# RWKV-7 layer on one core: separate decay loads, heads stacked alike and half-row Gram products in the recurrence, with re-timed planner tables

## The chip, the cores and the metric

The kernel runs on one core of a Trainium2 chip. The metric is the device time of one execution in microseconds, median of the runs; lower is better. The engines are named as in the profile: PE is TensorE, DVE VectorE, ACT ScalarE, POOL GpSimd, SP SyncE, which here only issues DMAs.

## The reference, cut to what matters

One layer (DEPTH is 1) over 2048 tokens of width 1024: RWKV-7 time mixing with 16 heads of 64, a LayerNorm, then a gated MLP of width 2816 with a causal convolution of width 3, and a second LayerNorm. The part that the change touches is the recurrence over time:

```python
def step(state, inp):
    r_t, w_t, k_t, v_t, kk_t, a_t = inp
    sa = jnp.einsum('bhij,bhj->bhi', state, -kk_t)
    state = (state * w_t[:, :, None, :]
             + sa[..., None] * (kk_t * a_t)[:, :, None, :]
             + v_t[..., None] * k_t[:, :, None, :])
    return state, jnp.einsum('bhij,bhj->bhi', state, r_t)
```

`w_t` is a decay per channel, the exponential of a negative decay log. All is float32.

## The kernel before

The program is one list of nodes. Each node has an engine, a cost in us (`dur`), a due time (`prio`), the nodes it depends on, and the buffers that it takes and gives back. A planner in the Python code (`Plan.order`) plays this list through with these costs, at each moment starts on a free engine the ready node with the lowest due time, and writes the instructions out in that order. On the chip each engine runs its own instructions strictly in the order written. So the numbers in `pl.add(engine, cost, due, ...)` and in the tables TS, TW and TF set the order in which instructions stand; they cost no time by themselves. A changed cost in one phase can reorder another, since the plan is one.

There are four phases, which overlap at their borders: the projections (A, to about 700 us), the recurrence (S, about 700 to 1280), the output projection with LayerNorm (W, to about 1490), and the MLP (F, four blocks of 512 tokens, to the end).

The recurrence goes over 16 tiles `t` of 128 tokens; a tile has two chunks `c` of 64 tokens and two halves `h` of 8 heads, and heads are taken in pairs, `e` being the even or the odd one. Per half:

- One DMA loads `l`, 128 x 5 x 512: r, kp, kkn, b and th (the decay logs); there is one buffer for it. PE sums the decay logs along the chunk (`csI`), and ACT makes three exponentials, `P`, `Pe` and `Pi`.
- DVE multiplies kkn by `Pe` (line 875) and r by `P` (line 879), PE transposes both (`tr`) and ACT writes them to `AR`. PE also transposes the whole of `P` (`pcp`), of which only two columns per pair, the chunk decays, are kept in `PC`.
- DVE multiplies b and kp by `Pi` into `BKn` (line 928). For even heads b lies in partitions 0 to 63 and kp in 64 to 127, for odd heads the other way round, so each multiply is split by `e`: 64 x 256 elements, in blocks of 64. PE transposes `BKn` (`tb`), and ACT copies each head's 64 rows into one of two tiles `BKT`, whose other 64 rows are kept zero; there is one pair of them.
- PE makes the Gram products `G`, 128 contraction rows of which 64 are zero, and DVE masks them into `Gm` (line 955).

Per tile DVE then inverts 64 small triangular matrices, 31 steps of a multiply and an add (lines 990 and 995), between DMAs that regroup them (`NU`, `NUs`, `XD`, `XT`). Per chunk follow the serial steps: ACT copies the state to `UV`, PE makes `Z`, `SA`, `dS` and the output `Y`, and DVE updates `stmp` (line 1141) and `state` (line 1146).

Of W this matters: for each tile ACT takes squares, DVE makes a reciprocal root (line 1295 and twelve short operations of lines 173 to 178), scales and gates (`wE`, lines 1312 and 1315), PE transposes (`tr`, line 1338), ACT and DVE split the result (`yH`, `yL`), and PE multiplies it into `z`. In F, PE alternates between `ps` (first matrix, weights split by DVE into `wiL`, line 1594) and `acc` (second matrix, weights split into `woL`, line 1559); each product is three passes, high x high, low x high, high x low, so `acc` needs `woL`. Between two blocks DVE also runs the final norm of one block (`xr`, lines 1687 and 1690) and prepares the residual of the next (`xr`, lines 1653 and 1654).

## Time and profile before

| | |
|---|---|
| median of 3 runs | 2953.81 us (2953.59 to 2956.54) |
| the profiled execution's own time | 2945.05 us |
| its span in the trace | 2943.1 us |
| mean granted PE clock in it | 0.984 |
| tiles of the recurrence | 16 |

The span is the time from the first to the last instruction in the trace. An engine's busy time is the union of its instructions; semaphore waits are not in it. A timeline row gives start and length; where two rows follow each other on an engine without a wait, the distance of their starts is what the first one costs.

### The profile page before, as it was taken

The page shows a single profiled execution, that of the slowest core. Times are in us where ns is not written, and L with a number is a line of the kernel's source. Part 1 is how long each engine was busy: PE and PEld are TensorE (multiplying, and loading weights), DVE is VectorE, ACT ScalarE, POOL GpSimd, SP SyncE. Part 2 cuts the span into 40 slices and gives each one's busy share as a digit, 9 for nine tenths or more (in the row PEclk, how much of TensorE's full clock was granted, in tenths as well). Part 3 has the DMA queues.
Part 4 walks back from the last instruction along what each step waited for, and adds up shares of the span by engine and source line. Part 5 has one row for each costly group of instructions (what it writes and reads, how often), then busy time and mean ns, then how long its engine had stood idle before and what let it go on. Part 6 is the DMA issues. An engine that isn't in the chain of part 4 may idle for free.

```text
span 2943.1 us, 51765 instructions
## 1 busy us (share of the span) xinstructions
PE 2803.2 (95%) x19392; PEld 2317.1 (79%) x19392; DVE 2086.2 (71%) x4288; ACT 1742.4 (59%) x4668; POOL 53.7 (2%) x96
## 2 busy tenths in 40 slices
PE   7998999998789999789999999999999999999997
PEld 5776778887677777678888888888888888888886
DVE  7888768986899999779865555475554745548454
ACT  8888657764578877887554444444444444444441
POOL 0000000001000000001100000000000000000000
PEclk9999999999899999899999999999999999999999
DMA  6446555435456656568652323343333432334222
GB/s 199 148 167 220 184 186 185 158 119 176 120 151 160 161 159 157 140 207 307 208 185 95 101 96 121 98 151 101 101 119 99 153 98 90 129 97 159 92 90 79
DMA packets 298555, 424.08 MB, mean 144 GB/s; under 512 B 153952, under 2 KB 179552, under 8 KB 294208
## 3 DMA queue, kind: packets, MB, share of 16 engines
q1 hardware_dynamic: 286976, 379.87, 41.3%
q0 software_dynamic: 11328, 40.90, 3.9%
q8 instruction: 153, 2.51, 0.4%
q14 instruction: 98, 0.80, 0.1%
HBM read 311.57 MB, written 109.12 MB: 143 GB/s over the span
## 4 chain that ended last, share of the span: by engine, by line
issue 55%; PE 21%; DVE 12%; ACT 7%; DMA 3%; POOL 1%; SPq 0%; POOLq 0%; ACTq 0%; DVEq 0%
PE ps L164 4%; PE ps L165 4%; PE ps L166 4%; DVE BKn L928 3%; ACT junk L643 2%; PE G L768 2%; DVE XU L995 2%; DVE itmp L990 2%; DVE Gm L955 1%; DMA l<-in 1%; PE Y L768 1%; DMA in<-av 1%; DVE l L879 1%; ACT junk L1283 1%; DVE l L875 1%
## 5 line engine op out<-in xcount | busy, mean ns | idle before, releaser
L166 PE MATMUL ps<-xH,wiL 128*128 128x512 f32 x1408 | 548.2, 389 | 0.5 <-DVE wiL L1594 0.5
L164 PE MATMUL ps<-xH,wiH 128*128 128x512 f32 x1408 | 548.1, 389 | 0.0
L165 PE MATMUL ps<-xL,wiH 128*128 128x512 f32 x1408 | 547.8, 389 | 0.0
L1594 DVE TENSOR_TENSOR wiL<-wis,wiH 128x1024 fp32r<-128x1024 f32 x176 | 215.4, 1224 | 459.0 <-ACT wiH L1455 459.0
L1455 ACT ACTIVATE hb<-ps 128x512 f32<-128x512 f32 x176 | 105.7, 601 | 484.4 <-PE ps L166 484.4
L164 PE MATMUL ps<-WH,xiH 128*128 128x512 f32 x768 | 305.1, 397 | 16.4 <-ACT xiH L255 9.5
L166 PEld LDWEIGHTS ps<-xH,wiL 128*128 128x128 f32 x1408 | 264.3, 188 | 56.9 <-DVE wiL L1594 2.1
L165 PEld LDWEIGHTS ps<-xL,wiH 128*128 128x128 f32 x1408 | 264.3, 188 | 54.8
L164 PEld LDWEIGHTS ps<-xH,wiH 128*128 128x128 f32 x1408 | 264.3, 188 | 54.6
L165 PE MATMUL ps<-WL,xiH 128*128 128x512 f32 x768 | 302.8, 394 | 2.2 <-DVE WL L350 2.2
L166 PE MATMUL ps<-WH,xiL 128*128 128x512 f32 x768 | 301.9, 393 | 0.0
L1622 DVE SCALAR_TENSOR_TENSOR cv<-hb,cw,cv 128x512 f32<-128x512 f32 x352 | 263.7, 749 | 19.9 <-ACT cv L1618 13.7
L165 PE MATMUL acc<-woL,aH 128*128 128x512 f32 x688 | 268.2, 390 | 2.2 <-DVE woL L1559 2.2
L164 PE MATMUL acc<-woH,aH 128*128 128x512 f32 x688 | 267.8, 389 | 0.0
L166 PE MATMUL acc<-woH,aL 128*128 128x512 f32 x688 | 267.7, 389 | 0.0
L1455 ACT ACTIVATE wiH<-wis 128x1024 fp32r<-128x1024 f32 x178 | 189.0, 1062 | 6.5 <-DMA wis<-in_w_in_dram 6.5
L164 PEld LDWEIGHTS ps<-WH,xiH 128*128 128x128 f32 x768 | 146.4, 191 | 54.6 <-ACT xiH L255 9.5
L1455 ACT ACTIVATE woH<-wos 128x512 fp32r<-128x512 f32 x172 | 108.7, 633 | 110.5 <-PE acc L166 103.9
L165 PEld LDWEIGHTS ps<-WL,xiH 128*128 128x128 f32 x768 | 146.3, 190 | 33.0 <-DVE WL L350 3.0
L166 PEld LDWEIGHTS ps<-WH,xiL 128*128 128x128 f32 x768 | 146.2, 190 | 31.2 <-DVE xiL L474 0.2
L165 PEld LDWEIGHTS acc<-woL,aH 128*128 128x128 f32 x688 | 129.1, 188 | 30.6 <-DVE woL L1559 4.0
L164 PEld LDWEIGHTS acc<-woH,aH 128*128 128x128 f32 x688 | 129.1, 188 | 27.4 <-ACT woH L1455 0.5
(243 smaller groups left out, 5349.3 us busy)
## 6 DMA issues: line engine op xcount, KB each, us to landing
wis<-in_w_in_dram SPq DMA_DIRECT2D x176, 512.0 KB
wos<-in_w_out_dram SPq DMA_DIRECT2D x172, 256.0 KB
l<-in SPq DMA_DIRECT2D x32, 1280.0 KB
xT<-in_xT_dram SPq DMA_DIRECT2D x21, 1028.0 KB
in<-kp SPq DMA_DIRECT2D x64, 256.0 KB
stg<-in_w_rkv_dram SPq DMA_DIRECT2D x48, 256.0 KB
gs<-gs SPq DMA_DIRECT2D x24, 512.0 KB
in<-kr SPq DMA_DIRECT2D x32, 256.0 KB
```

The costliest lines, as they stand in the source:

```text
L164: nc.tensor.matmul(ps, lH, rH, start=start, stop=False)
L165: nc.tensor.matmul(ps, lH, rL, start=False, stop=False)
L166: nc.tensor.matmul(ps, lL, rH, start=False, stop=stop)
L643: nc.scalar.activation(junk, Z["kr"][:, 64 * i:64 * i + 64], AF.Square, accum_out=st["ss"][:, tl, i:i + 1])
L768: MM = lambda out, l, r, **kw: nc.tensor.matmul(out, l, r, **{**dict(start=True, stop=True), **kw}, skip_group_check=True)
L875: TT(l[:, 2], l[:, 2], V[t]["Pe", h], op=OP.mult)
L928: TT(dst[rows, :, e], pe8(l[:, 1 if part else 3], e), pe8(V[t]["Pi", h], e), op=OP.mult)
L990: TT(V[t]["tv"], V[t]["XU"][:, 0:m, s:s + 1].to_broadcast([128, m, n]), V[t]["NUs"][:, s:s + 1, s + 1:32].to_broadcast([128, m, n]), op=OP ...
L995: TT(x, x, V[t]["tv"], op=OP.add)
L1455: CP = lambda out, in_, **kw: nc.scalar.activation(out, in_, AF.Copy, **kw)
L1594: TT(W["L"], W["s"], W["H"], op=OP.subtract)
L1622: STT(R[j], W["hb"][:, i:i + 512], C["cw"][:, fc, i:i + 1], R[j], op0=OP.mult, op1=OP.add)
```

## The change

In the recurrence: the stored layout becomes r, kkn, b, kp, th. The decay logs come by a DMA of their own into an own buffer (`th`), the other four by a second one (`l`, 128 x 4 x 512). `P` and `Pe` become one tile, and one multiply of 128 x 1024 (`f_MR`) replaces the two of lines 875 and 879. The chunk decays come from a product of `P` with two columns of the identity. b lies in partitions 0 to 63 and kp in 64 to 127 for all heads, so the `BKn` multiply is 64 x 512 and unsplit. `BKT` is one full tile, copied at once, with two buffers and no zeros; `G` uses the 64 rows of a head, alternating between upper and lower half. The top-left product of the inversion (`mp<-X,Gm`) reads rows 0 to 31 for both heads. `UV` gets v by two DMAs per tile in place of four. Buffers are allocated one by one, and given back earlier. Of TS the offsets within a tile change, of TW the due times of gating, transposes and loads, and node costs change in S, W and F. The diff, cut to its core:

```diff
-                    for i, q in enumerate(("r", "kp", "kkn", "b", "th")):
+                    for i, q in enumerate(("r", "kkn", "b", "kp", "th")):
...
-    TS = dict(hf=12, T=23.2, lds=5.0, hs=8.9, inv=31.0, mrg=66.3, mc=4.0, uv=47.5, st=70.2, cs=17.6, e0=30.0, p0=-3.4, fill=(), fn=1,
-              slots=dict(lds=1, pw=4, P=1, Pi=1, Pe=1, AR=4, BKn=4, Gm=4, PC=4, BKT=1, NUs=2, XU=2, XT0=1, XT1=1, X11=2, mp=1,
+    TS = dict(hf=12, T=23.2, lds=5.0, hs=7.55, inv=32.07, mrg=66.35, mc=4.0, uv=31.22, st=65.59, cs=17.34, e0=30.0, p0=-3.4, fill=(), fn=1,
+              slots=dict(cs=1, lth=1, lds=1, pw=4, P=1, Pi=1, AR=4, BKn=4, Gm=4, PC=4, BKT=2, NUs=2, XU=2, XT0=1, XT1=1, X11=2, mp=1,
...
-                    self.ld(tile_of(t, f"l{h}", ldp, [128, 5, 512], tag="lds"), self.S["in", t, h])
+                    self.ld(tile_of(t, ("th", h), ldp, [128, 512], tag="lth"), self.S["in", t, h][:, 4])
...
+                    self.ld(tile_of(t, f"l{h}", ldp, [128, 4, 512], tag="lds"), self.S["in", t, h][:, 0:4])
...
-                    TT(l[:, 2], l[:, 2], V[t]["Pe", h], op=OP.mult)
...
-                    TT(l[:, 0], l[:, 0], V[t]["P", h], op=OP.mult)
...
+                    l = V[t][f"l{h}"][:, 0:2]
+                    TT(l, l, V[t]["P", h], op=OP.mult)
...
-                        nc.tensor.transpose(pcp[:, p].rearrange("q c t -> q (c t)"),
-                                            V[t]["P", h][:, p * 128:(p + 1) * 128], self.ident)
+                        MM(pcp[:, p], V[t]["P", h][:, 0, p * 128:(p + 1) * 128], self.ident[:, 63:128:64])
...
-                            for e in range(2):
-                                rows = es(1 - e) if part else es(e)
-                                TT(dst[rows, :, e], pe8(l[:, 1 if part else 3], e), pe8(V[t]["Pi", h], e), op=OP.mult)
+                            TT(V[t]["BKn"][es(part), c, 8 * h:8 * h + 8].rearrange("q h i -> q (h i)"),
+                               V[t][f"l{h}"][es(c), 2 + part], V[t]["Pi", h][es(c)], op=OP.mult)
...
-                        for e in range(2):
-                            CP(x[e][es(e)], V[t]["tb", h, c][es(e)])
+                        CP(tile_of(t, ("BKT", h, c), wkp, [128, 4, 128], tag="BKT", bufs=sl["BKT"]), V[t]["tb", h, c])
...
-                                MM(G[:, p], V[t]["BKT", h, c][e][:, p],
-                                   V[t]["AR"][:, c, 4 * h + p].rearrange("q a t -> q (a t)"))
+                                MM(G[e][:, p], V[t]["BKT", h, c][es(e), p],
+                                   V[t]["AR"][es(e), c, 4 * h + p].rearrange("q a t -> q (a t)"))
...
-    TW = dict(ne=4, st=-31.5, gt=-31.1, tr=-14.5, ld=-22.0, out=26.9, p0=1000.0,
+    TW = dict(ne=4, st=-31.5, gt=-19.78, tr=-16.92, ld=-27.59, out=26.9, p0=1000.0,
...
-                    accs[h] = [pl.add("PE", 2.56, pr, lambda: [acc_mm(f, h, tl, R["H"], R["L"]) for tl in range(4)],
+                    accs[h] = [pl.add("PE", 2.73, pr, lambda: [acc_mm(f, h, tl, R["H"], R["L"]) for tl in range(4)],
...
-                    n_mm = pl.add("PE", 5.14, pr, f_mm, [n_w] + xn, take=("w_" + e,), give=("f_wi",))
+                    n_mm = pl.add("PE", 5.47, pr, f_mm, [n_w] + xn, take=("w_" + e,), give=("f_wi",))
```

The new tables move instructions in W and F too, where no operation changes. Two places matter below.

The first is DVE's queue where the recurrence ends and W begins. `q`, `rsw`, `rsy` and `rn` are the reciprocal root of one tile of W, `wE` its scaling and gating, `yE` the split of the transposed result, `stmp` and `state` the last updates of the recurrence. Before, the rows from the end of the second tile's root read:

```order
L178 SCALAR_TENSOR_TENSOR rn<-rsw,rsy 128x16
L1315 TENSOR_TENSOR wE<-wE 128x1024
L1312 TENSOR_TENSOR wE<-wE,rn 128x1024
L1257 TENSOR_TENSOR woL_16314<-wos,woH_16313 128x512
L1141 TENSOR_TENSOR stmp<-dS,state 128x256
L1315 TENSOR_TENSOR wE<-wE 128x1024
L1146 TENSOR_TENSOR state<-stmp,PC 128x256
L1141 TENSOR_TENSOR stmp<-dS,state 128x256
L1359 TENSOR_TENSOR yE_16034<-tr,yE_16034 128x512
L1146 TENSOR_TENSOR state<-stmp,PC 128x256
L1257 TENSOR_TENSOR woL_16505<-wos,woH_16504 128x512
L1315 TENSOR_TENSOR wE<-wE 128x1024
```

Now, from the end of the first tile's root (ahead of that root's twelve rows this queue has `stmp`, `state` and `X` rows of the recurrence alone):

```order
L178 SCALAR_TENSOR_TENSOR rn<-rsw,rsy 128x16
L1144 TENSOR_TENSOR state<-stmp,PC 128x256
L1139 TENSOR_TENSOR stmp<-dS,state 128x256
L1311 TENSOR_TENSOR wE<-wE,rn 128x1024
L1144 TENSOR_TENSOR state<-stmp,PC 128x256
L1314 TENSOR_TENSOR wE<-wE 128x1024
L1256 TENSOR_TENSOR woL_16017<-wos,woH_16016 128x512
L1314 TENSOR_TENSOR wE<-wE 128x1024
L1256 TENSOR_TENSOR woL_16071<-wos,woH_16070 128x512
L1294 TENSOR_SCALAR q<-q 128x16
```

Before, the roots of two tiles and half of their gating stood ahead of the recurrence's last four `stmp` rows, and the first splits `yE` between these. Now the first root stands behind all `stmp` rows but the last, the gating between and behind the last two `state` rows, then a second root (the row `q`), and the splits behind that.

The second is DVE's queue between the first two blocks of F: from the first `cv` pair behind the final norm's first operation to the pair of `woL` splits that the next block's first sums need. Before:

```order
L1631 TENSOR_TENSOR cv_22648<-cv_22648,cv_22748 128x512
L1687 SCALAR_TENSOR_TENSOR xr<-xr,bmv,g_19351 128x1024
L1638 TENSOR_TENSOR aL<-cv_22648,aH 128x512
L1690 SCALAR_TENSOR_TENSOR xr<-xr,brs,b_19353 128x1024
L1594 TENSOR_TENSOR wiL<-wis,wiH 128x1024
L1687 SCALAR_TENSOR_TENSOR xr<-xr,bmv,g_19351 128x1024
L1653 TENSOR_TENSOR xr<-xr,ag 128x1024
L1690 SCALAR_TENSOR_TENSOR xr<-xr,brs,b_19353 128x1024
L1654 TENSOR_TENSOR xr<-xr,ab 128x1024
L1559 TENSOR_TENSOR woL<-wos,woH 128x512 x2
L1653 TENSOR_TENSOR xr<-xr,ag 128x1024
L1622 SCALAR_TENSOR_TENSOR cv_22821<-hb,cw,cv_22821 128x512 x2
```

Now, from the two earlier `woL` splits to the same two:

```order
L1558 TENSOR_TENSOR woL<-wos,woH 128x512
L1689 SCALAR_TENSOR_TENSOR xr<-xr,brs,b_19189 128x1024
L1637 TENSOR_TENSOR aL<-cv_22485,aH 128x512
L1686 SCALAR_TENSOR_TENSOR xr<-xr,bmv,g_19187 128x1024
L1621 SCALAR_TENSOR_TENSOR cv_22632<-hb,cw,cv_22632 128x512 x2
L1689 SCALAR_TENSOR_TENSOR xr<-xr,brs,b_19189 128x1024
L1652 TENSOR_TENSOR xr<-xr,ag 128x1024 x2
L1653 TENSOR_TENSOR xr<-xr,ab 128x1024
L1558 TENSOR_TENSOR woL<-wos,woH 128x512
L1653 TENSOR_TENSOR xr<-xr,ab 128x1024
L1558 TENSOR_TENSOR woL<-wos,woH 128x512
```

Between the first operation of the final norm and the first of these two `woL` rows there is now one more pair of `cv` and one more `ag`; all else on that stretch is the same work in another order.

## Rows read from the trace of the kernel before

**Rows 1.** The page: the span, and each engine's busy time over it
```profile
span 2943.1 us, 51765 instructions
...
PE 2803.2 (95%) x19392; PEld 2317.1 (79%) x19392; DVE 2086.2 (71%) x4288; ACT 1742.4 (59%) x4668; POOL 53.7 (2%) x96
```

**Rows 2.** Busy time by window: start:end, length, each engine's, granted clock, DMA
```profile
...
700.00:750.00 50.00, 38.96 (x254) 32.94 (x253) 36.51 (x88) 23.29 (x73) 4.71 (x9) 0.86 0.55 163
850.00:900.00 50.00, 47.02 (x944) 40.36 (x937) 47.71 (x159) 42.44 (x86) 1.03 (x2) 1.00 0.63 165
1000.00:1050.00 50.00, 45.64 (x903) 38.95 (x904) 47.86 (x146) 39.63 (x81) 1.07 (x2) 1.00 0.64 162
1200.00:1250.00 50.00, 36.58 (x924) 33.14 (x918) 36.84 (x129) 40.27 (x114) 2.15 (x4) 0.83 0.65 157
```

**Rows 3.** Groups by form, VectorE, 850 to 1200 us: count | busy, mean ns | idle before
```profile
...
L928 DVE TENSOR_TENSOR BKn<-l,Pi 64x256 f32<-64x256 f32 x176 | 72.8, 419 | 3.3 <-ACT Pi L857 0.3
...
L879 DVE TENSOR_TENSOR l<-l,P 128x512 f32<-128x512 f32 x22 | 15.1, 684 | 1.1 <-ACT P L857 1.0
```

**Rows 4.** Timeline of VectorE in 900 to 935 us: start, length, operation
```profile
...
903.55 0.68 DVE L955 TENSOR_TENSOR Gm<-G,c_gmask 128x512 f32<-128x512 f32 x1
904.15 0.68 DVE L875 TENSOR_TENSOR l<-l,Pe 128x512 f32<-128x512 f32 x1
...
907.77 0.86 DVE L928 TENSOR_TENSOR BKn<-l,Pi 64x256 f32<-64x256 f32 x2
908.65 0.29 DVE L990 TENSOR_TENSOR itmp<-XU,NUs 128x126 f32<-128x126 f32 x1
```

**Rows 5.** Groups by form, TensorE, 850 to 1200 us
```profile
...
L768 PE MATMUL G<-AR,BKT 128*128 128x128 f32 x704 | 96.6, 283 | 0.0
...
L768 PE MATMUL Y<-state,AR 64*64 64x64 f32 x704 | 25.3, 221 | 0.4 <-ACT Yt L767 0.3
...
L768 PE MATMUL csI<-l,c_triI 128*128 128x512 f32 x44 | 22.9, 603 | 1.6 <-DMA l<-in 1.6
```

**Rows 6.** Waits in 700 to 860 us: who for whom, total us, times, longest
```profile
...
DVE Gm L955 <- PE G L768: 14.8, 10, 4.6
ACT BKT L767 <- PE G L768: 14.5, 10, 2.8
```

**Rows 7.** Timeline of VectorE in 1244 to 1300 us, recurrence's end
```profile
...
1252.48 0.17 DVE L1295 TENSOR_SCALAR q<-q 128x16 f32<-128x16 f32 x1 [3.60 <-ACT junk L1283]
...
1256.52 1.23 DVE L1312 TENSOR_TENSOR wE<-wE,rn 128x1024 f32<-128x1024 f32 x1
...
1267.00 0.42 DVE L1141 TENSOR_TENSOR stmp<-dS,state 128x256 f32<-128x256 f32 x1 [1.92 <-PE dS L768]
...
1278.87 0.42 DVE L1146 TENSOR_TENSOR state<-stmp,PC 128x256 f32<-128x256 f32 x1
```

**Rows 8.** Timeline of TensorE in 1240 to 1290 us
```profile
...
1265.24 0.66 PE L1338 MATMUL tr<-ident,wE 128*128 128x128 f32 x4
...
1275.39 0.50 PE L164 MATMUL z<-woH,yE 128*128 128x512 f32 x1
```

**Rows 9.** Timeline of VectorE in 1955 to 1976 us, between two blocks of the FFN
```profile
...
1957.96 1.28 DVE L1687 SCALAR_TENSOR_TENSOR xr<-xr,bmv,g 128x1024 f32<-128x1024 f32 x1
...
1962.76 1.54 DVE L1622 SCALAR_TENSOR_TENSOR cv<-hb,cw,cv 128x512 f32<-128x512 f32 x2
...
1971.33 1.22 DVE L1653 TENSOR_TENSOR xr<-xr,ag 128x1024 f32<-128x1024 f32 x1
1972.47 1.28 DVE L1690 SCALAR_TENSOR_TENSOR xr<-xr,brs,b 128x1024 f32<-128x1024 f32 x1
...
1974.80 1.29 DVE L1559 TENSOR_TENSOR woL<-wos,woH 128x512 fp32r<-128x512 f32 x2
```

**Rows 10.** Timeline of TensorE in 1975 to 1979 us
```profile
...
1976.07 0.39 PE L164 MATMUL acc<-woH,aH 128*128 128x512 f32 x1
1976.29 0.39 PE L165 MATMUL acc<-woL,aH 128*128 128x512 f32 x1
```

More of the change, by code (lines that the diff above doesn't have):

```diff
@@ L790, in f_open1 @@
             nbI, nbIn, nbE, scE = (cols[:, i:i + 1] for i in range(4))
-            for i in range(sl["BKT"]):
-                BKTs.append([wkp.tile([128, 4, 128], F32, name=f"BKT{i}{e}") for e in range(2)])
         def f_open2():
@@ L895, in s_nodes @@
+                pcs.append(pl.add("ACT", 0.1, hb + 0.8, f_pc, [n_pp] + (pcs[:1] or aw), take=() if h else ("PC",), give=("pw",)))
                 evs = []
                 trs = []
-                for i, n_x in ((0, n_M), (1, n_R)):
+                for i in range(2):
                     def f_tr(t=t, h=h, i=i):
-                        l = V[t][f"l{h}"]
                         ps = tile_of(t, ("tr", h, i), pw, [128, 4, 2, 64], tag="pw")
@@ L932, in f_tb @@
+                for c in range(2):
                     def f_tb(t=t, h=h, c=c):
@@ L958, in s_nodes @@
[L958 to L959 removed]
+                        grams.append(pl.add("DVE", 0.6, hb + 2.3 + c + 0.1 * e, f_gm, [n_g] + (grams[:1] or aw),
+                                            take=() if h + c + e else ("Gm",), give=("pw",)))
             e0 = (t == 0) * o["e0"]
@@ new lines, in s_nodes @@
+                    n_z = pl.add("PE", 1.08 * d, sp, f_z, [n_s0, n_ga[c]], take=bk)
+                    n_zs.append(pl.add("ACT", 0.49 if nh == 1 else 0.28, sp, f_zs, [n_z, prevA] + n_zs[-1:]))
+                    n_sa = pl.add("PE", 1.08 * d, sp, f_sa, n_zs[-1:] + [n_x12[c]], give=(f"XT{c}",) if lastu else ())
+                    n_su.append(pl.add("ACT", 1.23 if nh == 1 else 0.79, sp, f_su, [n_sa]))
+                    n_ds = pl.add("PE", 1.08 * d, sp, f_ds, n_su[-1:], give=("BKn",) if c and lastu else ())
@@ new lines, in s_nodes @@
+                    n_w.append(pl.add("DVE", 0.6 if nh == 1 else 0.33, sp, f_w, [n_ds, *prevS] + n_w[-1:], give=bk))
+                    n_s1.append(pl.add("DVE", 0.6 if nh == 1 else 0.33, sp, f_s1, n_w[-1:] + n_s1[-1:] + [prevY] + pcs,
+                                       give=("PC",) if c and lastu else ()))
+                n_y2 = pl.add("PE", 1.08, sb + 4.5, f_y2, n_su + [n_y1] + (n_s1 if c else []),
+                              give=("Gm", "UV") if c else ())
+                n_yt = pl.add("ACT", 1.22, sb + 5, f_yt, [n_y2], take=() if c else ("Yt",), give=("Y",))
```

214 lines of the change are left out of this document (100 added, 114 removed).

## The prediction

> **What bounds the kernel now.** I read the page first. PE is busy for 95% of the span and DVE for 71% [rows 1], but these are means over four phases. The table by windows separates them. From about 800 to 1200 us, in the recurrence, DVE is busy 47.7 to 47.9 of 50 us; the rest is gaps of a few ns between some 150 instructions. PE shows 45.6 to 47 of 50 there, but a matmul's end is modelled and overlaps the next one, and the clock is full [rows 2]. At the two ends of the recurrence neither engine is full (DVE 36.5 and 36.8 of 50) and the granted clock is down to 0.86 and 0.83 [rows 2]: there a chain of waits sets the time. The groups of DVE give the unit: 22 multiplies of line 879 in 350 us, two per tile, are 11 tiles, so a tile takes 31.8 us [rows 3]. The costliest group is the `BKn` multiply, 16 per tile.
>
> **The change, part by part, on DVE.** The `BKn` multiply: 16 of 64 x 256 per tile become 8 of 64 x 512. Two of them take 0.88 us from start to next start, 0.44 each [rows 4], so 7.04 us per tile. No row has the new form. From below, a 128 x 512 multiply costs 0.60 to the next start [rows 4]; from above, two old ones cost 0.88. Between these, a 128 x 1024 operation takes 1.14 [rows 9], so 512 further columns cost 0.54 and 256 further ones 0.27, which on top of 0.44 makes 0.71. I take 0.65, between 0.60 and 0.71, nearer to the contiguous row because the blocks of 64 go: 5.2 us per tile, 1.84 saved (0 to 2.24 at the bounds).
>
> The joined multiply: 0.60 + 0.60 becomes 1.14, twice per tile: 0.12 saved. All else on DVE (masks, inversion, transposes, updates) keeps its count. A tile of DVE falls by 1.96 to 29.9 us. DVE is the bound for some 14 of the 16 tiles; the first two are the filling, priced below: 14 x 1.96 = 27.4 us (1.7 to 33).
>
> **The filling.** In 700 to 860 us ACT waits ten times, 14.5 us, to write `BKT` until `G` is through with the only pair, and DVE ten times, 14.8 us, for `G` [rows 6]. With two buffers and one shorter `G` group, most of the first wait goes and DVE's follows it, since the two are the two ends of one loop. Ten times 0.9 of 1.45 us is 9 us; bounds 0 (DVE or the loads are late next) and 14.5.
>
> **PE and ACT.** `G` costs 96.6/704 = 0.137 us per pass of 128 columns, 64 passes per tile, 8.8 us. The `Y` product, whose two heads use the two halves of the rows, costs 25.3/704 = 0.036 for 64 columns, half of what 0.137 would give for them [rows 5]. So with heads alternating I take half, 4.4 us per tile saved; bounds 0 and 4.4. `pcp` on two columns may gain or lose a few tenths. None of it is on the bound: PE, at about 29 us of modelled busy time per tile, only has to stay under 29.9. Of eight 64-row `BKT` copies per tile four remain, of full height; ACT is busy 40 to 42 of 50 and not the bound [rows 2]. The separate `th` load is one more DMA per half on SP, and two `UV` loads per tile go, so SP issues as many as before. `l` still has one buffer; `csI` waited for it 1.6 us in 350 [rows 5], and with `th` ahead the exponentials no longer wait for the whole load, so I put the loads at 0.
>
> [...]
>
> **What the new order costs.** Where the recurrence ends, the first `z` product started at 1275.39, 3.5 us before DVE's last `state` at 1278.87, because the first root at 1252.48 and the gating at 1256.52 ran while DVE waited for the chain, up to the next `stmp` at 1267.00 [rows 7, 8]. In the new order the first root is queued behind a late `stmp`. After the last `state` two gating operations of 1.14 and a `woL` of 0.60 remain, 2.9 us; then PE transposes, 0.66 [rows 8]; the split comes behind a second root of twelve operations of some 0.2, so about 3 us more. `z` then starts 6.5 us after the last `state` in place of 3.5 before it: 10 us lost. Bounds: 0, if the tail's chain is late anyway, and 16.5, if transposes to `z` take the 10.1 us that they take now (1265.24 to 1275.39) on top of the 2.9.
>
> Between blocks of the MLP the pair of `woL` splits now comes 1.5 (a `cv` pair) + 1.14 (`ag`) = 2.6 us later, counted from the final norm's first operation at 1957.96 [rows 9]. The first `woL` was done at about 1975.5 (half of the pair's 1.29), and PE's first product that needs it started at 1976.29, right behind another [rows 9, 10]: 0.8 us of slack. So PE waits 1.8 us or more; with some of the slack used otherwise, 2.2, at three borders: 6.5 us (0 to 9). What is queued behind are PE's sums and then all of the next `ps`; PE's products follow each other without a gap there [rows 10], so this is lost for good.
>
> **The sum.** -27.4 - 9 + 10 + 6.5 = -19.9, say -20 us. Made against the profiled execution, 2943.1 of span and 2945.05 of its own time, it gives 2925; that execution was 0.3% under the median of the runs. Against the median, 2953.8 - 20 = 2934 us, 0.7% faster. What a measurement of this kernel tells from no change is about 0.2%, 6 us.
>
> **The rivals.**
>
> - *The new order costs nothing* (the tail's chain and DVE's slack hide both): -36, 2917 us. For it, DVE waited 3.6 us for `q`'s squares even before [rows 7]; against it, the queues are in order and the places are plain in the rows. Chance 0.12.
> - *A late load eats the gain.* One buffer for `l`, given back by the last `BKn` multiply: if DVE waits 0.7 us per half for the next, 14 x 1.4 = 20 us are gone and the time stays at about 2954. Against it, 1.6 us of waiting in 11 tiles [rows 5]. Chance 0.08.
> - *The wide multiply is no cheaper per element* (0.88 for 64 x 512): the steady part saves 1.7, and the sum is -1.7 - 9 + 16.5 = +6, 2960 us, slower. The sum turns where 14 x (7.16 - 8x) = 7.5, at x = 0.83 us per multiply. For it, two of the old ones show no overlap (0.86 for two of 0.43) [rows 4]; against it, the 128 x 512 one does. Chance 0.07.
> - *PE becomes the bound.* `G` halved leaves PE some 24.6 us per tile at full clock, if the pairs overlap. It then idles more, and where it was busy 39 and 37 of 50 us the granted clock was 0.86 and 0.83 [rows 2]; the new stage would show about 41. At a mean clock of 0.75 a tile takes 32.8, 14 x 1.0 = 14 more, and the sum is 14 - 9 + 16.5 = +21, 2975 us. It turns slower below about 0.79. Against it, PE's idle time is spread over many small groups. Chance 0.05. [...]
>
> **How the numbers follow.** Forecast 0.68. Its own range runs from the bounds that matter: `BKn` at 0.60 or 0.71 moves it by -6 or +7, the filling by -5 or +9, the handover and the borders by -16 or +9; taken together as independent about 2919 to 2948. To leave out no more than 2 in 10 the range takes in the first rival and half of the second: 2914 to 2952 us. Faster by over 0.2%: the forecast and the first rival, 0.80. Within 0.2%: the late load and the forecast's upper edge, 0.09. Slower: the other two, less their milder halves, 0.11.
>
> **What would show it.** Right: a tile every 29.9 us between 850 and 1150 with DVE still at 47 of 50; `BKn` with 8 per tile at 0.60 to 0.71 to the next start; `G` at half the PE time; no more waits of ACT for `G`; PE waiting for `wE` or `yE` where W begins; PE waiting about 2 us for `woL` three times in F. Wrong: DVE waits for `l` or `G` in the steady stage, a granted clock under 0.9 there, or a `BKn` multiply near 0.88.

## The result and the profile after

The changed kernel takes 2991.74 us, median of 4 runs (2985.95 to 2999.43), against 2953.70 (2945.82 to 2956.54) before: ratio 1.0144 [1.0127, 1.0160], 38 us slower. The prediction, 20 us faster, was wrong in sign. The profiled executions, 2990.03 against 2945.05 of their own time, have spans of 2987.9 and 2943.1: 44.8 us to be found.

The page, the line that answers to [rows 1]:

```profile
span 2987.9 us, 51767 instructions
...
PE 2806.7 (94%) x19520; PEld 2319.5 (78%) x19520; DVE 2054.0 (69%) x4128; ACT 1705.1 (57%) x4604; POOL 52.6 (2%) x94
```

DVE has 32 us less work and ACT 37 less, PE is level. So the work did fall, and the time went into waits. The windows, as in [rows 2]:

```profile
700.00:750.00 50.00, 38.17 (x298) 30.45 (x297) 38.57 (x79) 21.85 (x66) 4.70 (x9) 0.88 0.67 190
850.00:900.00 50.00, 43.37 (x870) 37.38 (x869) 40.17 (x120) 33.74 (x71) 0.53 (x1) 0.86 0.57 158
1000.00:1050.00 50.00, 45.37 (x855) 39.06 (x855) 43.50 (x141) 34.81 (x69) 0.53 (x1) 0.89 0.55 141
1200.00:1250.00 50.00, 33.98 (x762) 30.39 (x760) 42.18 (x155) 31.55 (x72) 2.14 (x4) 0.79 0.44 98
```

In the middle of the recurrence DVE fell from 47.8 to 40.2 and 43.5 of 50 and stopped being the bound, no engine took its place, and the granted clock fell from 1.00 to about 0.88. The length of a tile comes from the rows of one line in a stretch; of `state`, 860 to 1180 us, they give count, durations, and first and last start:

```profile
L1144 DVE TENSOR_TENSOR state<-stmp,PC x19: 682/684/686, 867.7 to 1172.8; 128x512 f32<-128x512 f32 x19
```

Two `state` rows are a tile, so 18 distances are nine tiles: 305.1 / 9 = 33.9 us, against 31.8 before and 29.9 forecast. Without its waits (idle stretches of over 0.15 us) a tile of DVE takes 29.4 us, against 31.6 before, worked out for both from the stretch between the first and the last of these rows: 2.2 us of work are saved, about as forecast, and 4.5 us of waits came in. The waits in 850 to 1200 us (total us, times, longest):

```profile
DVE stmp L1139 <- PE dS L768: 22.7, 9, 4.1
...
PE Y L768 <- ACT Yt L767: 18.6, 10, 2.3
...
PE csI L768 <- DMA th<-in: 11.8, 7, 3.3
...
DVE l L862 <- DMA l<-in: 7.8, 6, 2.5
```

Before, DVE's waits in 850 to 1150 us came to 0.2 us; now they come to 41. DVE is kept waiting mostly by PE, and PE by DMA and ACT. How one wait makes the next is seen in the timeline of PE, 920 to 934 us, and of DVE behind it:

```profile
927.37 2.04 PE L768 MATMUL csI<-th,c_triI 128*128 128x512 f32 x2 [1.86 <-DMA th<-in]
929.20 1.71 PE L768 MATMUL pcp<-ident,P 128*128 128x2 f32 x8
930.77 1.09 PE L895 MATMUL tr<-ident,l 128*128 128x128 f32 x4
931.79 1.98 PE L768 MATMUL dS<-UV,BKn 128*64 128x64 f32 x32
```

```profile
933.82 0.69 DVE L1139 TENSOR_TENSOR stmp<-dS,state 128x512 f32<-128x512 f32 x1 [2.63 <-PE dS L768]
```

The operands of `dS` (ACT's `UV`) were ready at 926.95. PE stood at `csI` for the late `th`, ran `pcp` and `tr` ahead of `dS` as the list says, and DVE waited 2.63 us for `dS`. Of the nine waits for `dS`, PE had stood for `th` shortly before in six; ahead of the two longest (3.0 and 4.1 us) it had stood 2.3 and 2.2 us inside a group of equal products with nothing awaited (last section). And `th` is late because of SP's queue, 944 to 954 us:

```profile
944.63 4.88 SPq L147 DMA_DIRECT2D XT<-XD  x8
949.62 1.12 SPq L147 DMA_DIRECT2D UV<-vc  x2
950.79 1.97 SPq L147 DMA_DIRECT2D NUs<-NU  x2
952.86 0.56 SPq L147 DMA_DIRECT2D l<-in  x1
953.46 0.49 SPq L147 DMA_DIRECT2D th<-in  x1
```

The product `csI` that gives the only `th` buffer back had started at 942.82. The next `th` load is issued 10.6 us later, behind sixteen other transfers. SP waits for less than 1 us of that: the rest is SP issuing them one after the other. The same happens once in every tile from 850 to 1200 us (16 or 17 transfers, 9.8 to 11.0 us); the load for the other half is issued 1.1 to 2.1 us after its `csI` started.

The handover, for [rows 7, 8], DVE and then PE:

```profile
1295.40 1.22 DVE L1311 TENSOR_TENSOR wE<-wE,rn 128x1024 f32<-128x1024 f32 x1
1296.53 0.42 DVE L1144 TENSOR_TENSOR state<-stmp,PC 128x256 f32<-128x256 f32 x1
1296.87 1.22 DVE L1314 TENSOR_TENSOR wE<-wE 128x1024 f32<-128x1024 f32 x1
...
1298.60 1.22 DVE L1314 TENSOR_TENSOR wE<-wE 128x1024 f32<-128x1024 f32 x1
```

```profile
1299.88 1.12 PE L1337 MATMUL tr<-ident,wE 128*128 128x128 f32 x4 [5.58 <-DVE wE L1314]
1303.47 1.12 PE L1337 MATMUL tr<-ident,wE 128*128 128x128 f32 x4 [2.47 <-DVE yE L1358]
1304.23 0.78 PE L164 MATMUL z<-woH,yE 128*128 128x512 f32 x1
```

The gating stands around and behind the last `state`; `z` starts 7.7 us after it, before 3.5 us ahead of it.

The first border of F, for [rows 10], and the windows around it:

```profile
2007.89 0.80 PE L165 MATMUL acc<-woL,aH 128*128 128x512 f32 x1 [3.33 <-DVE woL L1558]
2008.49 0.63 PE L166 MATMUL acc<-woH,aL 128*128 128x512 f32 x1
2008.91 0.63 PE L164 MATMUL acc<-woH,aH 128*128 128x512 f32 x1
```

```profile
2004.50:2007.50 3.00, 0.06 (x1) 0.00 (x0) 2.62 (x3) 0.50 (x1) 0.00 (x0) 0.97 0.75 229
2007.50:2011.00 3.50, 3.11 (x8) 2.48 (x9) 3.50 (x5) 0.00 (x0) 0.00 (x0) 0.54 0.57 169
2011.00:2014.50 3.50, 3.50 (x17) 2.91 (x16) 3.46 (x5) 1.27 (x2) 0.00 (x0) 1.00 0.85 286
```

PE stands 3.33 us for `woL` and then runs at half clock (0.50 granted from 2007.5 to 2010.5): a product of 512 columns takes 0.63 in place of 0.39.

Where the 44.8 us went, by landmarks that both traces have:

| landmark | before | after | later by | so this stretch lost |
|---|---|---|---|---|
| second `state` (filling) | 802.4 | 808.0 | 5.6 | 5.6 |
| 24th `state` (eleven tiles on) | 1163.3 | 1184.6 | 21.2 | 15.6 |
| last `state` | 1278.9 | 1296.5 | 17.7 | -3.5 |
| first `z` of W (handover) | 1275.4 | 1304.2 | 28.8 | 11.1 |
| first `ps` of F | 1483.6 | 1511.6 | 28.0 | -0.8 |
| last `ps` of F, behind its three borders | 2859.1 | 2904.1 | 45.0 | 17.0 |
| end of the span | 2943.1 | 2987.9 | 44.8 | -0.2 |

### The profile page after: what moved, and what is told of

Same layout as the page of the kernel before. It is cut to its first block, busy times and chain, and to the rows that moved or that the text cites. A ratio compares the mean times of both kernels' runs of the same rounds, so it can differ in the third digit from the quotient of the medians.

```text
span 2987.9 us, 51767 instructions
## 1 busy us (share of the span) xinstructions
PE 2806.7 (94%) x19520; PEld 2319.5 (78%) x19520; DVE 2054.0 (69%) x4128; ACT 1705.1 (57%) x4604; POOL 52.6 (2%) x94
## 4 chain that ended last, share of the span: by engine, by line
issue 55%; PE 23%; DVE 8%; ACT 7%; DMA 5%; POOL 1%; SPq 1%; POOLq 0%; ACTq 0%; DVEq 0%
PE ps L164 4%; PE ps L165 4%; PE ps L166 4%; ACT junk L643 3%; DMA th<-in 2%; DVE BKn L923 1%; DVE itmp L989 1%; PE G L768 1%; DVE XU L994 1%; PE dS L768 1%; PE csI L768 1%; DVE Gm L956 1%; DMA in<-av 1%; PE Y L768 1%; PE pcp L768 1%
## 5 line engine op out<-in xcount | busy, mean ns | idle before, releaser
L165 PE MATMUL acc<-woL,aH 128*128 128x512 f32 x688 | 270.8, 394 | 12.7 <-DVE woL L1558 12.7
```

The lines of the kernel that those rows point to most:

```text
L165: nc.tensor.matmul(ps, lH, rL, start=False, stop=False)
```

## The experiments

The theory after this reading: DVE's work fell, but the new order and the loads let waits in, above all a late `th` and `l`. The rivals: the granted clock, because PE idles; the tables of W and F; DVE being the bound still, with a wide multiply of no use. Ratios are to the kernel before. "Last `state`" is that row's start in the profiled execution (before 1278.9, after 1296.5).

**g_twice: PE kept busier**, for the clock.

```diff
-                        for p in range(4):
+                        for p in [0, 0, 1, 1, 2, 2, 3, 3]:
```

> The changed kernel with each G product issued twice into the same place (the result is the same, PE has about 4.4 us more work per tile). Three theories stand. CLOCK: the halved G leaves PE idle more often, the granted clock falls to half for 25 us of the 350 between 850 and 1200 us, and every chain through PE gets longer. By it the extra work keeps PE busy, the clock there goes from 0.88 to 0.97 or more, a tile falls from 34.2 us to 31.5 or less, and the time falls by some 25 to 35 us, to about 2960. LOADS: the single buffers of l and th set the pace (a load is issued only when the last BKn multiply or csI has given its buffer back, and takes 7 to 9 us); PE falls asleep while it waits for th, so the clock is a consequence. By it more PE work does not help: 2985 to 3010, with the same waits for th and l. ORDER: 28 of the 45 us come behind the recurrence (handover and block borders) and don't move here by either theory.

Measured: 3012.77 us, 1.0208 [1.0190, 1.0227], last `state` 1320.3. The window 850 to 1150:

```profile
850.00:1150.00 300.00, 263.66 (x5394) 231.19 (x5390) 246.22 (x743) 199.28 (x404) 4.80 (x9) 0.95 0.55 147
```

The clock rose from 0.88 to 0.95, and the time by 21 us. Here the added work went with a higher clock. PE's time for `G` grew from 49.6 to 81.5 us in 850 to 1200 us, 3.4 us per tile or some 55 in all, of which 21 came through: PE's work is partly on the chain now. (The 25 us at half clock in the expectation are too few: of the 350 us in after, 82 ran at half clock, which is the mean of 0.88.)

**l_split: `l` in two loads**, r and kkn given back after the transposes, b and kp after the last `BKn`.

```diff
-                    self.ld(tile_of(t, f"l{h}", ldp, [128, 4, 512], tag="lds"), self.S["in", t, h][:, 0:4])
+                    self.ld(tile_of(t, f"l{h}", ldp, [128, 2, 512], tag="lds"), self.S["in", t, h][:, 0:2])
+                def f_load2(t=t, h=h):
+                    self.ld(tile_of(t, f"k{h}", ldp, [128, 2, 512], tag="ldk"), self.S["in", t, h][:, 2:4])
```

> The changed kernel with the load of r, kkn, b, kp split in two halves of 512 KB with a buffer each: the half of r and kkn is given back by the second group of tr transposes, that of b and kp by the last BKn multiply. LOADS: the round trip of the buffer that the joined multiply waits for loses the BKn multiplies (some 6 us), DVE's waits for l and PE's for th go, a tile falls from 34.2 to 31 or less, the clock rises with it, and the time falls by 30 to 45 us, to 2947 to 2962. CLOCK: nothing of PE's work changes; the granted clock stays at 0.88 between 850 and 1200, a tile at 33.5 to 34.5, and the time within 8 us of 2992.

Measured: 2970.28 us, 1.0064 [1.0040, 1.0087], last `state` 1278.2. More than half of the loss is gone, with a clock of 0.89 in the middle, as after.

**old_wf: the table TW and the costs of W and F as before**, the recurrence's untouched.

```diff
-    TW = dict(ne=4, st=-31.5, gt=-19.78, tr=-16.92, ld=-27.59, out=26.9, p0=1000.0,
+    TW = dict(ne=4, st=-31.5, gt=-31.1, tr=-14.5, ld=-22.0, out=26.9, p0=1000.0,
...
-                    n_mm = pl.add("PE", 5.47, pr, f_mm, [n_w] + xn, take=("w_" + e,), give=("f_wi",))
+                    n_mm = pl.add("PE", 5.14, pr, f_mm, [n_w] + xn, take=("w_" + e,), give=("f_wi",))
```

> The changed kernel with the table of offsets and the planner's costs of everything behind the recurrence (TW, the final projection, the MLP) as they were before. ORDER: the handover (+11 us) and the three block borders (+17 us with the clock's fall behind each) go, and the time falls by 22 to 30 us, to about 2965; the recurrence stays as it is, 34.2 us per tile. If instead the handover is late because the recurrence ends late and PE is at half clock there, the borders alone go, and the time falls by 17, to about 2975.

Measured: 2983.42 us, 1.0105 [1.0083, 1.0126]. PE's waits for `woL` in F fell from 12.7 us to 1.6, and the borders lost nothing. The handover kept its 6.4 us from the last `state` to `z`, so the table alone does not make it. The last `state` was at 1311.5. Up to 1190 us every engine runs the operations of after in the order of after, and yet the 24th `state` starts 9.9 us later. From the second to the 24th it took 384.3 us, against 376.6, and PE stood inside groups with nothing awaited (last section) for 19.9 us of that, against 11.6: where the order is the same, these stalls account for the difference.

**th_two: two buffers for `th`.**

```diff
-              slots=dict(cs=1, lth=1, lds=1, ...
+              slots=dict(cs=1, lth=2, lds=1, ...
```

> The changed kernel with two buffers for th, so that its load no longer waits for the csI before it. LOADS, in the form that th is the late one: PE's waits for th (11.8 us in ten tiles, in front of pcp, tr and dS in its queue) go, a tile falls from 34.2 to 32.5 to 33, and the time falls by 15 to 25 us. LOADS in the form that l is the late one: DVE's waits for l stay, and the time falls by no more than 8. CLOCK: with PE's longest sleeps gone the clock rises a little; under 10 us.

Measured: 2971.08 us, 1.0064 [1.0044, 1.0085], last `state` 1278.2. DVE's waits for `dS` in 850 to 1150 fell from 18.6 us to 3.8, those for `l` rose from 7.8 to 13.8: one late load was hidden behind the other. This edit and l_split also move other rows in the planner's order, and PE stood some 5 us less inside groups in both, so neither gives the price of its load alone.

**combo: l_split, th_two and old_wf together.**

> The changed kernel with the split load (r, kkn / b, kp), two buffers for th, and the old offsets and costs behind the recurrence, together. LOADS and ORDER: the split and the second th buffer each took about 18 us from the recurrence, so together they take 18 (if they cure the same wait) to 35 (if two), and the old costs take the 17 us of the block borders: 2940 to 2957. If DVE is the bound again once the loads are hidden, a tile comes down to 30 to 31 us with DVE busy 47 of 50. CLOCK: if PE's half clock keeps the tile long by itself, the tile stays at 32 to 32.5 with the clock at 0.9, and the time at 2955 to 2960.

Measured: 2957.41 us, 1.0026 [1.0014, 1.0039], last `state` 1274.4, `z` at 1278.3. That is 13 us under either load edit, and old_wf alone was 8 under after: the two load edits add at most 5 to each other, as if they cured the same chain.

**combo_half: combo with `BKn` in two multiplies of 64 x 256 each.**

```diff
+                            for e in range(2):
+                                u = slice(256 * e, 256 * e + 256)
+                                TT(V[t]["BKn"][...][:, u], V[t][f"k{h}"][es(c), part, u], V[t]["Pi", h][es(c), u], op=OP.mult)
```

> The kernel of the run before in this list (split load, two th buffers, old order behind the recurrence), with each BKn multiply of 64 x 512 cut into two of 64 x 256: DVE has about 1.4 us more work per tile, 20 us in all. If DVE is the bound of the steady stage, the time rises by some 20 us over that run; if the chain of loads and of PE is, DVE has the time to spare, and it rises by less than 6.

Measured: 2965.04 us, 1.0064 [1.0047, 1.0081]: 7.6 us longer. The two halves cost 0.38 each to the next start here, 0.76 a pair against 0.69 for the one, so the edit added 0.57 us per tile, some 9 us in all, and most of it came through. So this run doesn't show that DVE has slack in combo. That it still waits there is seen in its rows: it is busy 267.5 of the 300 us from 850 to 1150, and waits 2.3 us per tile.

**before_th: the kernel before with `th` in an own load and one buffer**, and nothing else.

```diff
-                    self.ld(tile_of(t, f"l{h}", ldp, [128, 5, 512], tag="lds"), self.S["in", t, h])
+                    self.ld(tile_of(t, f"l{h}", ldp, [128, 4, 512], tag="lds"), self.S["in", t, h][:, 0:4])
+                def f_lt(t=t, h=h):
+                    self.ld(tile_of(t, ("th", h), ldp, [128, 512], tag="lth"), self.S["in", t, h][:, 4])
```

> The kernel before with one part of the change alone: th in a load of its own with one buffer, ahead of the load of the other four; heads, G, multiplies, offsets as before. LOADS: a single th buffer, given back by csI and queued on SP among the other loads, makes PE wait for th here as well: slower by 5 to 25 us. DVE BOUND: DVE is busy 47.9 of 50 us and sets the pace, and the exponentials only come earlier: within 6 us of before.

Measured: 2988.42 us, 1.0140 [1.0126, 1.0155], last `state` 1312.6. This one edit, with the order that the planner makes of it, costs 40 us, as much as the whole change. But it isn't a late `th`: in 850 to 1150 us PE waits for `th` once. DVE's own rows stay at 31.7 us per tile, and its waits stand at the inversion:

```profile
DVE itmp L994 <- DMA NUs<-NU: 10.5, 5, 3.8
DVE itmp L994 <- ACT BKT L767: 8.5, 2, 4.4
...
PE csI L768 <- DMA th<-in: 1.7, 1, 1.7
```

So `th` doesn't come late to `csI` here: the loads of `NUs` come late, which stand behind loads of `UV`, `th` or `l` in SP's queue in this order. What the load costs by itself isn't separated from that order.

**combo_junk: combo with two further products of 512 columns ahead of each `csI`.**

```diff
+                    for _ in range(2):
+                        MM(ps, triI, xui)
                     MM(ps, triI, V[t]["th", h])
```

> The combined kernel (split load, two th buffers, old order behind the recurrence) with two further 128 x 512 products of constants into csI's own bank right ahead of each csI; their result is overwritten, and they cost PE some 2 us per half, 4 us per tile. CLOCK: they keep PE busy where it slept, the granted clock between 850 and 1150 goes from 0.93 to 0.98 or more, and the time falls by 5 to 15 us. PE CHAIN: PE stands in order ahead of the products that DVE waits for, and the work costs more than the clock gives back: slower by 10 to 40 us, as the doubled G was.

Measured: 2997.50 us, 1.0165 [1.0150, 1.0180], 40 us over combo, at a clock of 0.94, where combo had 0.93. The junk hardly moved the clock, so this run doesn't test it; it shows that more work on PE ahead of `csI` makes the kernel longer.

**combo_ts: combo with TS's offsets of before** (`hs=8.9, inv=31.0, uv=47.5, st=70.2` and so on).

> The combined kernel with the offsets of the recurrence (hs, inv, mrg, uv, st, cs) as before the change. If the new offsets cost part of the steady stage, the time falls by 5 to 15 us; if they are right for the new pieces, it rises by 5 or more; if the order is set by what comes free and not by the offsets, within 5.

Measured: 2958.32 us, 1.0032 [1.0020, 1.0045]: no difference from combo that is clear of noise. What an offset is worth depends on the rest of the plan (before_off, below).

**combo_root: combo with the squares of W's first tile priced low**, so that the planner puts its root ahead of the last `stmp` rows.

```diff
-                n = pl.add("ACT", 0.54, PR(t) + o["st"], ...
+                n = pl.add("ACT", 0.05 if t < 1 else 0.54, PR(t) + o["st"], ...
```

> The combined kernel with the planner's price of the first tile's squares lowered, which moves the first root and the first gating on DVE ahead of the last pairs of stmp and state, as they stood before the change. ORDER, by the handover term of 10 us: the first z product comes 5 to 10 us earlier, and the time is 2948 to 2952, level with before. If the tail's chain is late anyway: within 3 us of the combined kernel.

Measured: 2950.91 us, 1.0007 [0.9995, 1.0018]: level with before, and the best of the changed kernels; `z` starts at 1274.4. The price moves the first two roots, their gating and W's splits behind them; up to 1180 us the order is that of combo. From the last `state` to the first `ps` of F it takes 204.2 us, against 216.1 in combo and 204.7 in before: the place of these rows is what the handover hung on. The window 850 to 1150:

```profile
850.00:1150.00 300.00, 259.20 (x5161) 219.92 (x5161) 268.12 (x814) 214.87 (x436) 4.78 (x9) 0.94 0.62 155
```

DVE is still 20 us under the 288 of before.

**joint: the changed kernel with `th` back in one load of five rows**, and old_wf's tables.

```diff
-                n_lt = pl.add("SP", 1.0, lb - 0.3, f_lt, [n_o1], take=("lth",), lat=3.5)
-                n_l = pl.add("SP", 3.0, lb, f_load, [n_o1], take=("lds",), lat=4.0)
+                n_l = n_lt = pl.add("SP", 3.0, lb, f_load, [n_o1], take=("lds",), lat=4.0)
```

> The changed kernel with th back in the one load of a half (five rows, 1.28 MB, one buffer, as before the change), and the old offsets and costs behind the recurrence, by which the first root stands ahead of the last pairs again. Stacked heads, half-row G, joined multiply, two-column decays and the new offsets of the recurrence stay. If the load of th alone did the damage, the recurrence ends where the combined kernel had it or earlier (last state at 1274 us or before), DVE's saving of 1.3 us per tile shows at last as 10 to 20 us, and the time is 2930 to 2942, below before. If the wait for a half's load, 7 to 8 us behind the last BKn multiply, is a bound of its own at 31.8 us per tile, the time is 2945 to 2957. CLOCK: with PE's sleeps left as they are, 2965 or more.

Measured: 2986.83 us, 1.0128 [1.0106, 1.0149], last `state` 1317.5. So the changed work can lose as much without the separate load. But this is another order too: DVE's own rows take 32.5 us per tile here, against 29.4 in after, so the run doesn't say what the load costs in after. In the mean a half goes round in 17.3 us: load 7.9 (from its issue to `csI`), `csI` and exponentials 3.4, multiplies up to the last `BKn` 6.0; 34.6 for a tile. The kernel before goes round the same loop in 15.8 (7.5, 2.3 and 5.9).

**joint_ts: joint with TS's offsets of before.**

> The run before in this list with the recurrence's offsets (hs, inv, mrg, uv, st, cs) as before the change too: what is left of the change are the stacked heads, the half-row G products, the joined multiply and the two-column decays. If the new offsets belong to the load of th alone, this is 3 to 10 us faster than the run before in this list; if they carry a gain of their own, slower by as much; else within 3.

Measured: 2990.06 us, 1.0139 [1.0112, 1.0167]: no cure.

**before_lite: the kernel before, loading four of the five rows** (r is left out, its place filled from kp).

```diff
-                    TT(l[:, 0], l[:, 0], V[t]["P", h], op=OP.mult)
+                    TT(l[:, 0], l[:, 1], V[t]["P", h], op=OP.mult)
```

> The kernel before with four of a half's five rows loaded (1.02 in place of 1.28 MB): r is left out, and its place is computed from the row of kp. The order on PE, DVE and ACT is unchanged. ROUND TRIP: each load lands about 1 us earlier, two per tile, and a tile falls from 31.8 us towards the 30.5 us of DVE's own work: faster by 10 to 20 us. DVE BOUND: DVE's operations follow each other with gaps of a few ns, the load lands early and waits: within 4 us of before.

Measured: 2947.88 us, 0.9993 [0.9983, 1.0003]. A fifth fewer bytes per load gave nothing, in this window:

```profile
850.00:1150.00 300.00, 276.05 (x5317) 235.94 (x5312) 288.12 (x928) 243.92 (x488) 4.80 (x9) 1.00 0.57 144
```

In the order of before, DVE was the bound and the loop of the loads was not.

**pool_ld: combo_root with the three loads on POOL's queue and the store of `Y` on SP's.**

```diff
-                n_lt = pl.add("SP", 1.0, lb - 0.3, f_lt, [n_o1], take=("lth",), lat=3.5)
+                n_lt = pl.add("POOL", 1.0, lb - 0.3, f_lt, [n_o1], take=("lth",), lat=3.5)
```

> The combined kernel with the first root early, and with the three loads of a half (l, k, th) issued by POOL, whose queue holds nothing else in the recurrence; the store of Y goes to SP in exchange. SP QUEUE: the loads no longer stand behind NU, XT and UV (up to 13 us), so they land before they are wanted, the waits of DVE and PE for them go, a tile falls from 32.2 to 30 to 31 us, and the time falls by 15 to 30 us to 2920 to 2937, below before. PE CHAIN: if the products and evictions of the state set the tile, the time stays within 6 us of 2951.

Measured: 2957.99 us, 1.0025 [1.0015, 1.0036].

**pool_only: the same, with the store of `Y` left on POOL.**

> The run before in this list, but with the store of Y left on POOL, where it waits for Yt ahead of later loads. SP QUEUE: the same gain as in that run if the store stands behind the loads it could block, less than half of it if the loads now wait behind the store; PE CHAIN: within 6 us of 2951.

Measured: 2954.19 us, 1.0012 [1.0000, 1.0024]. Neither beats combo_root: with two `th` buffers and a split `l`, taking loads off SP's queue gains nothing.

**gsplit: combo_root with `G` made for the even heads, then for the odd ones**, in place of alternating halves.

```diff
-                            for e in range(2):
-                                MM(G[e][:, p], V[t]["BKT", h, c][es(e), p],
+                                MM(G[:, p], V[t]["BKT", h, c][es(e), p],
```

> The combined kernel with the first root early, with the half-row G products issued as one group per head parity, each in one PSUM bank of its own, as before the change (the pairs no longer alternate between the two row halves). BANKS: G no longer needs two of the four banks of pw at once, and DVE's masks start after half a group; a tile falls from 32.2 to 31 us or less, faster by 10 to 20 us. PAIRS: the products lose the overlap of the two row halves, PE has some 4 us more per tile, and the time rises by 10 to 40 us, as with the doubled G.

Measured: 3050.71 us, 1.0340 [1.0325, 1.0355], 100 us over combo_root. The passes of `G` in 850 to 1200 us, in after and then here, and DVE's wait for `G` here in 850 to 1150:

```profile
L768 PE MATMUL G<-AR,BKT 64*128 64x128 f32 x672 | 49.6, 296 | 0.0
```

```profile
L768 PE MATMUL G<-AR,BKT 64*128 64x128 f32 x608 | 94.8, 315 | 0.0
```

```profile
DVE Gm L960 <- PE G L768: 38.0, 38, 3.1
```

A pass costs 0.156 us here, against 0.074 in after and 0.078 in combo_root: without the alternation a pass takes about twice as long. That makes 5.0 us per tile, some 80 of the 100; the order differs too.

**before_cost: the kernel before, with the planner's prices of the recurrence as in the changed one.** No operation, buffer, offset or load is touched.

```diff
-                n_ci = pl.add("PE", 0.86, hb, lambda f=f_cs: f(tri=triI, nm="csI"), [n_l] + [n_c] * (t == 0), take=("pw",))
+                n_ci = pl.add("PE", 1.06, hb, lambda f=f_cs: f(tri=triI, nm="csI"), [n_l] + [n_c] * (t == 0), take=("pw",))
...
-                    n_bt = pl.add("ACT", 0.96, hb + 2.1 + c, f_bt, [n_tb, n_z1], take=("BKT",), give=("pw",))
+                    n_bt = pl.add("ACT", 1.21, hb + 2.1 + c, f_bt, [n_tb, n_z1], take=("BKT",), give=("pw",))
```

> The kernel before with the planner's prices of the recurrence's steps as the changed kernel has them, and nothing else changed: every operation is as before, only their order on the engines moves. ORDER: the order before was one that fits DVE's full stage, and a like shift of prices costs a good part of what the change lost in the recurrence, 15 to 40 us. WORK: the same operations take the same time, DVE stays the bound at 31.8 us per tile, and the time is within 6 us of before.

Measured: 3003.10 us, 1.0182 [1.0165, 1.0199], last `state` 1322.2. The order alone costs 52 us, more than the whole change. Its window, and DVE's waits in it:

```profile
850.00:1150.00 300.00, 260.90 (x4772) 223.02 (x4770) 274.65 (x839) 221.24 (x444) 4.79 (x9) 0.96 0.54 146
```

```profile
DVE itmp L990 <- DMA NUs<-NU: 4.7, 2, 2.7
DVE Gm L955 <- PE G L768: 3.9, 7, 1.3
```

The waits are 11 us of 300; the rest is DVE's own rows, 33.3 us per tile in place of 31.6. Where before interleaves the inversions of two tiles, more steps here stand right behind the one that they need (last section): 61% of the steps have ended before the next row starts, against 41% in before. So the order costs by another way than in after, where DVE's own rows are short (28%) and it waits.

**before_off: the kernel before with TS's offsets of the changed one.**

```diff
-    TS = dict(hf=12, T=23.2, lds=5.0, hs=8.9, inv=31.0, mrg=66.3, mc=4.0, uv=47.5, st=70.2, cs=17.6, e0=30.0, p0=-3.4, fill=(), fn=1,
+    TS = dict(hf=12, T=23.2, lds=5.0, hs=7.55, inv=32.07, mrg=66.35, mc=4.0, uv=31.22, st=65.59, cs=17.34, e0=30.0, p0=-3.4, fill=(), fn=1,
```

> The kernel before with the new offsets of the recurrence (hs, inv, mrg, uv, st, cs) and nothing else changed. ORDER: slower by 10 us or more, from waits of DVE in the steady stage that the trace before does not show. WORK: within 6 us of before.

Measured: 2972.93 us, 1.0077 [1.0061, 1.0094], last `state` 1311.4. The offsets by themselves cost 22 us on the old kernel, again by DVE's own rows (33.5 us per tile), and nothing on combo.

## Why the prediction was wrong, step by step

**The step that failed** is "A tile of DVE falls by 1.96 to 29.9 us. DVE is the bound for some 14 of the 16 tiles", the term of -27.4. Its first half holds: 31.6 to 29.4 us of own work. Its second half took for granted that DVE, the bound before, would still wait for nothing. In its place 4.5 us of waits per tile came in, above all for `dS`, because PE was late: it stood for `th` at `csI`, and inside groups with nothing awaited. A tile takes 33.9 us, and the stage lost 15.6 us over eleven tiles where 22 of gain stood. Even in before DVE was full for some eleven tiles (850 to 1200 us), not 14: in 1200 to 1250 it was busy 36.8 of 50 [rows 2].

The prediction weighed order at the two ends of the recurrence and took it for neutral in the middle. before_cost (+52 us) and before_off (+22), which change no operation, show that it isn't. They lose mostly by longer rows of DVE, though, and after loses by waits; that the order made the waits of after is argued, not shown. How its loss divides between late loads, order and PE's stalls stays open: nine stalls with 11.6 us in all fall into the stretch that lost 15.6, old_wf says that they come through one for one, but combo_ts has 9.9 us of them in 850 to 1150 and isn't slower than combo with 1.5.

**"I put the loads at 0"** failed with it. `csI`'s 1.6 us of waiting in 350 was read as slack of the load; but the one `th` buffer is asked for again behind `NU`, `XT`, `UV`, `NUs` and `l` in SP's queue, and their issue alone takes some 10 us. The load edits each give back about 21 us (l_split, th_two), and 34 with the old tables of W and F (combo), each in another order than after's. before_th and joint lose as much in ways of their own, before_th with PE waiting for `th` once, so neither prices the load. The rival of the late load came nearest; it named `l`, where more of the waiting is for `th`, and put its price, 20 us, only as high as the gain.

**The `BKn` multiply**: 0.60 us to the next start for one of four and 0.72 for three (last section), 0.69 in the mean, where 0.65 was taken. The old price of 0.88 for two was one of the dearer pairs; the mean of the old form is 0.43 each. So the multiplies saved 16 x 0.43 - 8 x 0.69 = 1.3 us per tile, not 1.84, inside the bounds. That the tile's work still fell by 2.2 is luck for this term: the inversion steps got shorter, 0.219 to 0.204 us from start to start, 62 of them, which was not forecast (fewer stand behind the step that they need).

**The filling**, -9 forecast, +5.6 measured. ACT's waits for `G`, 14.5 us, are gone as said; DVE's stayed (11.5 of 14.8), and 7.4 us of waiting for `l` came in: the loads were late next, which stood there as the bound of 0. It came out beyond that.

**`G`**: 49.6 us for 672 passes in 850 to 1200 us, 0.074 each, about half of 0.137: right, and without the alternation gsplit measured 0.156. It was off the bound, as said.

**The handover**: +10 forecast, +11.1 measured, by the rows foretold. old_wf left it there, combo_root took it away by moving the roots with their gating and splits.

**The borders**: right in place and mechanism, mis-sized: 2.2 us each was taken, 3.33, 3.48 and 3.97 were waited, 10.8 in all, and the half clock behind each brings the loss to 17.0: 13.7 us of F ran at half clock (0.50 granted), none in before. Of each wait, a part isn't PE's delay by the order but DVE itself waiting for a transfer ahead of the `woL` split, 1.62, 1.75 and 2.17 us:

```profile
2004.88 1.23 DVE L1652 TENSOR_TENSOR xr<-xr,ag 128x1024 f32<-128x1024 f32 x1 [1.62 <-DMA xr<-xn]
...
2007.15 0.68 DVE L1558 TENSOR_TENSOR woL<-wos,woH 128x512 fp32r<-128x512 f32 x1
```

Without it 1.7 to 1.8 us remain, which is the 2.6 less 0.8 of the prediction; this wait and the clock are the two terms that it lacked. The granted clock was 0.97 in the window ahead of the first border's products, 0.54 in the one from 2007.5 to 2011 and 1.00 in the next; the prediction did not count it here.

**The clock rival** saw the clock fall, to 0.88. But g_twice raises it to 0.95 and is slower, and l_split gains 21 us at 0.89. So it goes with the waits rather than makes them; its own price isn't isolated.

**The range**: from the prediction's own terms the low end of its own range comes to 2916, not 2919; nothing hangs on it.

**Open**: combo_root has some 2 us less DVE work per tile than before, most of the late loads cured, W and F as before, and is only level. DVE still idles 32 us of 300 there, in small waits for `NUs` (4.7), `l` (5.6), `stmp` (3.5), `k` (2.6) and others; no engine is full. An order as tight as that of before for this work was not found, so whether the change can gain stays open. No version beat the kernel before.

## What to carry to other kernels

A saving on the engine that is the bound counts only as long as every other queue still meets it in time: where the order comes from a planner, price the order too, by running the old work in the new order and the new work with the old numbers. For a buffer that exists once, count from the instruction that frees it to the issue of its next load, with the issue of all that stands between on that queue, rather than the wait that shows today. Where busy time falls on every engine and the span grows, follow one wait back through the queues before blaming any engine.

## What was not expected of the hardware

**Dependent neighbours on DVE cost 0.12 us more.** Steps of the inversion in joint, where one tile's steps follow each other and each needs the one ahead, and then in before, where two tiles' steps alternate (timelines of DVE):

```profile
1007.60 0.24 DVE L988 TENSOR_TENSOR itmp<-XU,NUs 128x78 f32<-128x78 f32 x1
1007.88 0.24 DVE L993 TENSOR_TENSOR XU<-XU,itmp 128x78 f32<-128x78 f32 x1
1008.03 0.67 DVE L922 TENSOR_TENSOR BKn<-l,Pi 64x512 f32<-64x512 f32 x1
```

```profile
928.01 0.34 DVE L990 TENSOR_TENSOR itmp<-XU,NUs 128x78 f32<-128x78 f32 x2
928.29 0.34 DVE L995 TENSOR_TENSOR XU<-XU,itmp 128x78 f32<-128x78 f32 x2
```

In joint the next step starts 0.28 us after the first, 0.03 after its end, and the unrelated `BKn` behind it 0.09 before the end. In before, a row marked x2 holds one step of each tile, here of 128x78 and of 128x30; the unrelated step starts 0.16 us after that of 128x78, 0.08 before its end. So a neighbour that needs the step costs 0.12 us more. Over the 62 steps of a tile the mean from start to start is 0.219 in before, 0.204 in after, 0.245 in before_cost and 0.253 in joint: (0.245 - 0.219) x 62 = 1.6 us, nearly all of before_cost's 1.7 per tile.

**The new `BKn` multiply has two prices.** DVE in after:

```profile
928.00 0.68 DVE L923 TENSOR_TENSOR BKn<-l,Pi 64x512 f32<-64x512 f32 x1
928.60 0.26 DVE L989 TENSOR_TENSOR itmp<-XU,NUs 128x108 f32<-128x108 f32 x1
928.89 0.69 DVE L923 TENSOR_TENSOR BKn<-l,Pi 64x512 f32<-64x512 f32 x1
929.61 0.27 DVE L994 TENSOR_TENSOR XU<-XU,itmp 128x108 f32<-128x108 f32 x1
```

In each half from 850 to 1150 us the first of the four takes 0.60 to 0.61 to the next start and the other three 0.71 to 0.73; neither neighbour depends on it. By the code the first is the only one that both reads and writes from partition 0 on, as its neighbours do. No run tests whether that makes the difference.

**PE stalls inside a group, behind loads of kind `instruction`.** In after, groups of equal products stop seven times in 850 to 1150 us, for 0.4 to 2.4 us, 8.3 us in all, with nothing awaited that the trace names; in before they never do. The longest, on PE:

```profile
957.50 1.14 PE L768 MATMUL SA<-Zs,XT 64*64 64x64 f32 x31
961.07 0.21 PE L768 MATMUL SA<-Zs,XT 64*64 64x64 f32 x1 [2.42 <-issue]
```

On the DMA queue of kind `instruction` a load of 16 KB ran from 958.54 to 959.57, 1.5 us ahead of the stall's end. Each of the seven stalls ends 1.4 to 1.6 us after the end of such a load, of which there are 40 in these 300 us, one in 7.5 us. So it looks as if PE stood there for its own instructions; this is read off the times, and no run tests it. Why before has no such stall is not shown.
